# RWKV-7 systems: joined loads, stores and inverse tiles, and the lower triangles stored from ScalarE

## The chip, the cores and the metric

The kernel runs on one core of a Trainium2 chip, as one launch. The metric is device time in microseconds, the median of three runs. TensorE (PE; its weight loads are listed as PEld), VectorE (DVE), ScalarE (ACT) and GpSimd (POOL) compute; SyncE (SP) issues the DMAs in this kernel. All of them run their own instructions in order and wait for each other by semaphores.

## What is computed

One inference step of a two-layer decoder trunk in float32: layer 0 is a gated DeltaNet, layer 1 is RWKV-7 time mixing. 1104 tokens go through it at once: 8 sequences of 8 sample tokens, 16 meta tokens, and 1024 prompt tokens. The change touches layer 1 only. Its recurrence, per head of 64 channels:

```python
kk = l2norm((k * k_k).reshape(B, T, H, N))
k = k * (1.0 + (a - 1.0) * k_a)
decay = jnp.exp(-jnp.exp(w))
b_h = kk * a_h
def step(S, inp):
    S = (S * d_t[:, :, None, :]
         + jnp.einsum('bhvk,bhk->bhv', S, -kk_t)[..., None] * b_t[:, :, None, :]
         + v_t[..., None] * k_t[:, :, None, :])
    return S, jnp.einsum('bhvk,bhk->bhv', S, r_t)
```

It is followed by a GroupNorm per head, a bonus term, a SiLU gate, the output projection and a final RMSNorm. The states of both token mixers are outputs too.

## The kernel before

Tokens lie along the free axis in three segments of 384, 384 and 336 (`SEGS`). 64 tokens form a chunk, two heads of 64 channels fill the 128 partitions as one of 8 pairs, so a segment of a pair has 6 chunks and there are 24 items: item n is pair n mod 8 of segment n div 8. Within a chunk, the recurrence is solved through the inverse of a unit lower triangular 64x64 matrix per head, which the text calls a system.

Layer 1 has three parts.

*Keys, decays and rates* (`keys_decay_rate`, line 1165). For each pair, the k projection and the two low-rank paths give k, the running sum of log decays cs, and the rate a. Each is stored in DRAM (`kd`, `csd`, `ad`, each 8 x 128 x 1152) and read back later.

*Systems beside projections* (`layer1`, line 1801). A list `todo` holds 24 projections: r, v and z (m = 0, 2, 3) of 8 pairs. A projection (`project`, line 1152) loads two weight tiles on SP, splits each into a high and a low part (ACT, then POOL or DVE, `split`, line 82), runs its products on PE, copies the result on ACT and stores it by SP in `rd`, `vd` or `zd`. After the projections n = 1, 4, 7, 10 and 13, `rwkv_inverse` (line 1293) is called for a batch b of five items (the last batch has four).

For each item of a batch, `rwkv_inverse` takes the tiles `cs`, `a`, `k`, which were loaded one item ahead by `rwkv_load`, three DMAs with two buffers each (tiles `sldcs`, `slda`, `sldk`). ACT makes kk (`skk`, line 1268) and the decays and their inverses (`sDp`, `siD`, lines 1277 and 1278). DVE makes α, kk times the decay (`sal`, one buffer, line 1285), POOL mends its chunk heads (1286, 1288), POOL and DVE turn kk into bk, kk times a times the inverse decay (1310, 1311). SP stores α in `ald` and bk in `bkd` (1312, 1313). PE multiplies bk by α for 12 chunk-heads into `fL`, and the squares of kk by the half mask `hmask` into `frss`, two partitions by 384. ACT copies `fL` to `sgl` (1322); in segment 0 POOL masks the sample chunk (1324); SP stores it in `rltd` (1325). DVE copies the sums of squares (`rkc`, 1327) and SP stores them in `rssd` (1328).

After the last item, `block_scale` (line 489) reads `rssd` back as a column and as a row of blocks (`invR`, `bblk`), and `inverse_blocks` (line 457) inverts all 32x32 diagonal blocks of the batch at once on DVE: the blocks are read into `invA`, one block a partition, 62 DVE instructions (`invtmp`, `invT`, lines 452 and 454) work one after the other, and the result goes to DRAM (`r_u`, `r_t`) to be read back in matrix layout, as `T1n` (line 480) and as the diagonal blocks of each item's `sTT` (line 486: four loads per item). A `sTT` tile holds one item, 6 chunks by 64; there are three buffers, and two memsets (484) clear a corner of each before its loads. `inverse_merge` (line 506) then makes the off-diagonal block of each item: PE products `mY` and `mU`, a DVE scaling between them, an ACT copy after them. POOL scales the finished `sTT` (1336) and SP stores it in `ttd` (1337).

*The wave* (`wave`, line 1841). Systems and projections being done, the items go through the chunk recurrence as a skewed wave with PE's order written by hand. `rwkv_front` (line 1340) prepares an item: five loads (`fldcs`, `fldk`, `flda`, one buffer each, `fldr`, `fldv`, two each), α and bk from `ald` and `bkd` into `AR` and `BK` (1360, 1361), the inverse from `ttd` into `rTT` (1351). In segment 0, the sample states are read (`sn`, eight loads, line 1588) and written (`out_s_rwkv`, eight stores, 1636) for each pair.

The tile framework places the semaphores from the tiles' uses, and orders each engine's instructions by a planning pass over the whole program, save PE in the wave. A DMA issue takes its place in the order of the engine that issues it.

Of the kernel before, what the change touches and what calls it, by code (L numbers as in the profile page):

```python
# [11 lines left out]
ALU = mybir.AluOpType  # L12
# [23 lines left out]
class Builder:  # L36
# [76 lines left out]
    def consts(self):  # L113
# [15 lines left out]
        self.hmask = t(cp, [128, 2], "hmask")  # L129
        nc.gpsimd.memset(self.hmask, 0.0)  # L130
        for h in (0, 1):
            nc.gpsimd.memset(self.hmask[64 * h:64 * h + 64, h:h + 1], 1.0)
# [324 lines left out]
    def inverse_blocks(self, name, ltd, scale_blk, pool, TT, T1n, L21, nth):  # L457
# [7 lines left out]
        A = self.t(pool, [128, 1024], "invA", 2)[0:nb]  # L465
# [746 lines left out]
    def rwkv_masks(self, ap, first=False):  # L1212
# [14 lines left out]
        if first:  # L1227
            self.m_strs2 = t(ap, [128, 64], "m_strs2")
            mask(self.m_strs2, True)
            return  # L1230
# [17 lines left out]
    def rwkv_open(self):  # L1248
        self.rk2 = self.t(self.cp, [128, 144], "rk2")
        self.csd, self.ad, self.rd, self.vd, self.zd, self.kd = (self.dram([8, 128, 1152], n) for n in  # L1250
                                                                 ("csd", "ad", "rd", "vd", "zd", "kd"))
        self.ttd, self.ald, self.bkd = (self.dram([24, 128, 384], n) for n in ("ttd", "ald", "bkd"))

    def rwkv_load(self, n, pool, tag, names):
# [4 lines left out]
        for nm in names:  # L1259
            d = {"cs": self.csd, "a": self.ad, "r": self.rd, "v": self.vd, "k": self.kd}[nm]  # L1260
            ld[nm] = t(pool, [128, 384], tag + "ld" + nm, 2 if nm in "rv" or tag == "s" else 1)
            nc.sync.dma_start(ld[nm], d[p][:, c0:c0 + 384])
        return ld

    def rwkv_keys(self, p, ld, pool, tag):

        nc, t = self.nc, self.t
        kk = t(pool, [128, 384], tag + "kk", 2)
# [3 lines left out]
    def rwkv_decays(self, ld, pool, tag):  # L1272
# [4 lines left out]
        self.act(Dp[:, 1:385], ld["cs"], AF.Exp, scale=-self.DEC)  # L1277
        self.act(iD, ld["cs"], AF.Exp, scale=self.DEC)
# [14 lines left out]
    def rwkv_inverse(self, b, pool):  # L1293
# [4 lines left out]
        ltd, ssd = self.dram([nth, 128, 64], f"rltd{b}"), self.dram([nth, 128], f"rssd{b}")  # L1298
        for q, n in enumerate(items):
            s, p = divmod(n, 8)  # L1300
            names = ("cs", "a", "k")
# [6 lines left out]
            al = t(pool, [128, 6, 64], "sal", 1)  # L1308
            self.alpha(al, kk, Dp, s, nc.vector)
            nc.gpsimd.tensor_tensor(kk, kk, ld["a"], op=ALU.mult)  # L1310
            nc.vector.tensor_tensor(kk, kk, iD, op=ALU.mult)
            nc.sync.dma_start(self.ald[n], al.rearrange("p c k -> p (c k)"))
            nc.sync.dma_start(self.bkd[n], kk)
            gp = self.ps("f", 2, "L")
            ssp = self.ps("f", 2, "rss")
            for c in range(6):
                for h in (0, 1):
                    a = 64 * h
                    self.mm(gp[a:a + 64, 64 * c:64 * c + 64], kk[a:a + 64, 64 * c:64 * c + 64], al[a:a + 64, c, :])
            self.mm(ssp[0:2, 0:384], self.hmask, sq)  # L1320
# [656 lines left out]
```

## Time and profile before

| | us |
|---|---|
| median of three runs | 2365.65 (2362.40 to 2366.57) |
| the profiled execution | 2362.64 |
| its span, first to last instruction | 2360.9 |
| PE busy in the span | 2167.1 (92%) |
| DVE busy | 1571.2 (67%) |
| ACT busy | 1282.6 (54%) |
| POOL busy | 949.4 (40%) |

The page also gives the mean granted clock of TensorE, 0.964 of full speed, and 308.89 MB moved by DMA, 131 GB/s on average. All DMA issues of the program come from SP.

How to read the lines below. A group line has the kernel line, engine, operation, the tiles it writes and reads (`out<-in`, with the first letter of a PSUM tag in front of a PSUM tile's name, so `fL` is tile `L` in the banks tagged `f`), their shapes, the count, and times. A line of a tile's view has the shortest, median and longest instruction in ns, then the first and last start in us. `SPq` marks an issue on SP's queue; its time is that of the issue, not of the transfer. A wait line has who waited, for whom, the total in us, how often, and the longest. `issue` as a releaser means that the profile shows nothing that the engine waited for. In a timeline, a row is start, duration, and in brackets the engine's idle time just before and what ended it. PE's busy time is modelled from pipelined matmuls and includes time at a lower clock.

### The profile page before, as it was taken

How to read it: one execution, taken by the hardware profiler on the slowest of the kernel's cores; microseconds unless marked ns; L12 is line 12 of the kernel's file. 1: busy time of each engine (PE TensorE's matmuls, PEld its weight loads, DVE VectorE, ACT ScalarE, POOL GpSimd, SP SyncE). 2: the span in 40 equal slices, each digit the busy share in tenths (PEclk: the TensorE clock that was granted, in tenths of full speed). 3: DMA queues.
4: the chain of work that ended last, by engine and by line, in shares of the span. 5: the costliest groups of instructions: out<-in, count | busy, mean ns of one | idle time of the engine just before them, and what ended most of it. 6: DMA issues, size and time to landing. Idle time of an engine off the chain costs nothing. (4 is left out here: it accounts for less than half of the span.)

```text
span 2360.9 us, 54503 instructions
## 1 busy us (share of the span) xinstructions
PE 2167.1 (92%) x19737; PEld 1961.9 (83%) x19737; DVE 1571.2 (67%) x4219; ACT 1282.6 (54%) x3599; POOL 949.4 (40%) x1318
## 2 busy tenths in 40 slices
PE   6989999999999999999999999999888888899886
PEld 5888989889898989898989998887777866778775
DVE  6878677685858686774345833479878456667754
ACT  5455545564656555456333746646444355677763
POOL 3445333443435353434232523446445423344433
PEclk9999999999999999999999999998999998999998
DMA  3423332323233333335152145577774654677753
GB/s 113 107 76 104 88 94 78 101 75 105 78 101 91 90 102 88 109 90 184 48 163 83 52 163 175 182 199 197 188 181 130 178 160 143 178 220 227 215 153 126
DMA packets 499719, 308.89 MB, mean 131 GB/s; under 512 B 208089, under 2 KB 484826, under 8 KB 499450
## 3 DMA queue, kind: packets, MB, share of 16 engines
q1 hardware_dynamic: 499450, 305.41, 45.6%
q8 instruction: 156, 2.56, 0.5%
q14 instruction: 113, 0.93, 0.1%
HBM read 209.97 MB, written 95.33 MB: 129 GB/s over the span
## 5 line engine op out<-in xcount | busy, mean ns | idle before, releaser
L90 POOL TENSOR_TENSOR wlo<-wraw,whi 128x512 fp32r<-128x512 f32 (+2 forms) x252 | 332.4, 1322 | 359.8 <-ACT whi L86 334.4
L76 PE MATMUL d<-xc,whi 128*128 128x384 f32 (+2 forms) x910 | 260.2, 344 | 8.1 <-ACT whi L86 3.6
L86 ACT CAST whi<-wraw 128x512 fp32r<-128x512 f32 (+2 forms) x252 | 151.7, 603 | 138.8 <-PE dq L76 50.7
L419 DVE SCALAR_TENSOR_TENSOR cvy<-raw,cw,cvy 128x408 f32<-128x408 f32 (+2 forms) x288 | 178.3, 632 | 15.7 <-ACT cvy L62 13.8
L452 DVE TENSOR_TENSOR invtmp<-invA,invT 72x31 f32<-72x31 f32 (+31 forms) x403 | 172.7, 429 | 18.7 <-POOL invT L447 8.0
L76 PEld LDWEIGHTS d<-xc,whi 128*128 128x128 f32 (+1 forms) x910 | 168.9, 193 | 15.2 <-ACT whi L86 4.7
L454 DVE TENSOR_TENSOR invT<-invT,invtmp 72x31 f32<-72x31 f32 (+31 forms) x403 | 172.3, 428 | 6.6
L76 PE MATMUL dz<-xc,whi 128*128 128x384 f32 (+1 forms) x480 | 149.4, 343 | 0.0
L76 PE MATMUL dv<-xc,whi 128*128 128x384 f32 (+1 forms) x480 | 146.8, 335 | 0.0
L76 PE MATMUL d<-xa,whi 128*128 128x384 f32 (+3 forms) x450 | 141.4, 348 | 4.1 <-DVE xa L90 2.8
L76 PE MATMUL d<-xc,wlo 128*128 128x384 f32 (+2 forms) x428 | 143.9, 345 | 0.7 <-POOL wlo L90 0.7
L868 POOL TENSOR_SCALAR Sb<-Sb,eglb 128x128 f32<-128x128 f32 x128 | 80.4, 645 | 87.6 <-DMA Sb<-in_state_gdn 36.6
L76 PE MATMUL dz<-xa,whi 128*128 128x384 f32 (+1 forms) x288 | 100.3, 348 | 0.0
L76 PE MATMUL dv<-xa,whi 128*128 128x384 f32 (+1 forms) x288 | 99.9, 347 | 0.1
L76 PEld LDWEIGHTS d<-xa,whi 128*128 128x128 f32 (+1 forms) x450 | 85.2, 194 | 12.8 <-issue 5.2
L76 PEld LDWEIGHTS dz<-xc,whi 128*128 128x128 f32 x480 | 89.5, 192 | 0.8
L76 PEld LDWEIGHTS dv<-xc,whi 128*128 128x128 f32 x480 | 88.6, 188 | 0.5 <-issue 0.4
L76 PE MATMUL d<-xa,wlo 128*128 128x384 f32 (+3 forms) x252 | 86.6, 344 | 0.0
L62 ACT ACTIVATE o<-rA,gcol 128x128 f32<-128x128 f32 x128 | 46.6, 372 | 72.6 <-DVE S L779 72.0
L76 PE MATMUL d<-xh,wlo 128*128 128x384 f32 (+1 forms) x256 | 83.9, 343 | 2.0 <-POOL wlo L90 2.0
L76 PEld LDWEIGHTS d<-xc,wlo 128*128 128x128 f32 (+1 forms) x428 | 82.1, 194 | 4.0 <-issue 1.9
L76 PE MATMUL d<-xh,whi 128*128 128x384 f32 (+1 forms) x256 | 84.5, 344 | 0.5 <-ACT whi L86 0.5
(509 smaller groups left out, 7012.3 us busy)
## 6 DMA issues: line engine op xcount, KB each, us to landing
wraw<-in_gdn_w_in SPq DMA_DIRECT2D x96, 256.0 KB
wraw<-in_rwkv_w_rkvz SPq DMA_DIRECT2D x80, 256.0 KB
Sb<-in_state_gdn SPq DMA_DIRECT2D x64, 256.0 KB
wraw<-in_rwkv_w_o SPq DMA_DIRECT2D x40, 256.0 KB
E<-drow SPq DMA_DIRECT2D x24, 384.0 KB
attn<-drow SPq DMA_DIRECT2D x24, 384.0 KB
wraw<-in_gdn_w_out SPq DMA_DIRECT2D x36, 256.0 KB
out_s_gdn<-Sb SPq DMA_DIRECT2D x32, 256.0 KB
```

Source lines behind the costliest of these rows:

```text
L62: return self.nc.scalar.activation(out, in_, func, bias=bias, scale=scale, **kw)
L76: self.nc.tensor.matmul(out, lhsT, rhs, start=start, stop=stop)
L86: nc.scalar.copy(hi, x)
L90: e.tensor_tensor(lo, x, hi.bitcast(F32), op=ALU.subtract)
L419: nc.vector.scalar_tensor_tensor(y[:, 0:wd], raw[:, k:k + wd], cw[k], y[:, 0:wd], op0=ALU.mult, op1=ALU.add)
L452: nc.vector.tensor_tensor(tmp, A[:, j, j + 1:32].unsqueeze(2).broadcast_to([nb, n, m]), Tv[:, j, 0:m].unsqueeze(1).broadcast_to([nb, n, m] ...
L454: nc.vector.tensor_tensor(Tv[:, j + 1:32, 0:m], Tv[:, j + 1:32, 0:m], tmp, op=ALU.subtract)
L868: nc.gpsimd.tensor_scalar(Sb[:, u], Sb[:, u], self.eglb[:, hv, 4 * g + u:4 * g + u + 1], None, op0=ALU.mult)
```

## The change

Five edits, all in layer 1:

1. The DRAM copies of cs, a and k become one tensor `cakd` (8 x 128 x 3 x 1152), and those of r and v one tensor `rvd`. Writers use slices as before; `rwkv_load` reads all three (two) in one DMA into one tile. The system loads one tile per item instead of three, the front two instead of five.
2. α and bk share one SBUF tile `ab` (tag `sal`, one buffer) and one DRAM tensor `abd`; one store after bk replaces the two. `kk` has one buffer instead of two.
3. The sums of squares: `hmask` has 32 columns, three products of 128 columns write partitions 0, 32 and 64 of one bank, one copy of 96x128 puts them in a tile `kc` for the whole batch, and six stores after the batch's last item write `rssd`.
4. The store of the lower triangles to `rltd` is issued from ScalarE for segments 1 and 2 and stays on SP for segment 0, whose sample chunk POOL masks.
5. One tile `TA` of 30 chunks with one buffer takes the place of the items' `sTT`; `inverse_blocks` fills it by four loads and two memsets per batch. `invA` has one buffer instead of two. `rwkv_inverse` is called after the projections 0, 3, 6, 9 and 12.

```diff
-        A = self.t(pool, [128, 1024], "invA", 2)[0:nb]
+        A = self.t(pool, [128, 1024], "invA", 1)[0:nb]
...
-        self.csd, self.ad, self.rd, self.vd, self.zd, self.kd = (self.dram([8, 128, 1152], n) for n in
-                                                                 ("csd", "ad", "rd", "vd", "zd", "kd"))
-        self.ttd, self.ald, self.bkd = (self.dram([24, 128, 384], n) for n in ("ttd", "ald", "bkd"))
+        self.cakd, self.rvd, self.zd = (self.dram([8, 128, n, 1152], m) for n, m in ((3, "cakd"), (2, "rvd"), (1, "zd")))
+        self.csd, self.ad, self.kd = (self.cakd[:, :, x] for x in range(3))
+        self.rd, self.vd = (self.rvd[:, :, x] for x in range(2))
+        self.zd = self.zd[:, :, 0]
+        self.ttd, self.abd = self.dram([24, 128, 384], "ttd"), self.dram([24, 128, 768], "abd")
...
-        for nm in names:
-            d = {"cs": self.csd, "a": self.ad, "r": self.rd, "v": self.vd, "k": self.kd}[nm]
-            ld[nm] = t(pool, [128, 384], tag + "ld" + nm, 2 if nm in "rv" or tag == "s" else 1)
-            nc.sync.dma_start(ld[nm], d[p][:, c0:c0 + 384])
+        for g in names:
+            d = {"cak": self.cakd, "rv": self.rvd}[g]
+            x = t(pool, [128, len(g), 384], tag + "ld" + g, 1 if g == "cak" and tag == "f" else 2)
+            nc.sync.dma_start(x, d[p][:, :, c0:c0 + 384])
+            for j, nm in enumerate(g):
+                ld[nm] = x[:, j]
...
+        kc = t(pool, [96, 5, 128], "rkc", 1)
...
-            al = t(pool, [128, 6, 64], "sal", 1)
+            ab = t(pool, [128, 2, 384], "sal", 1)
+            al, bk = ab[:, 0].rearrange("p (c k) -> p c k", k=64), ab[:, 1]
             self.alpha(al, kk, Dp, s, nc.vector)
             nc.gpsimd.tensor_tensor(kk, kk, ld["a"], op=ALU.mult)
-            nc.vector.tensor_tensor(kk, kk, iD, op=ALU.mult)
-            nc.sync.dma_start(self.ald[n], al.rearrange("p c k -> p (c k)"))
-            nc.sync.dma_start(self.bkd[n], kk)
+            nc.vector.tensor_tensor(bk, kk, iD, op=ALU.mult)
+            nc.sync.dma_start(self.abd[n], ab.rearrange("p x k -> p (x k)"))
...
-            self.mm(ssp[0:2, 0:384], self.hmask, sq)
+            for g in range(3):
+                self.mm(ssp[32 * g:32 * g + 32, 0:128], self.hmask, sq[:, 128 * g:128 * g + 128])
...
-            nc.sync.dma_start(ltd[6 * q:6 * q + 6].rearrange("c q i -> q c i"), gl)
-            kc = t(pool, [2, 384], "rkc", 1)
-            nc.vector.tensor_copy(kc, ssp[0:2, 0:384])
-            nc.sync.dma_start(ssd[6 * q:6 * q + 6].rearrange("c (h i) -> h c i", h=2), kc.rearrange("h (c i) -> h c i", c=6))
+            (nc.sync if s == 0 else nc.scalar).dma_start(ltd[6 * q:6 * q + 6].rearrange("c q i -> q c i"), gl)
+            nc.vector.tensor_copy(kc[:, q], ssp[0:96, 0:128])
+        sv = ssd.rearrange("(q g c) (h i) -> g h q c i", g=3, c=2, h=2)
+        for g in range(3):
+            for h in (0, 1):
+                nc.sync.dma_start(sv[g, h:h + 1], kc[32 * g + h:32 * g + h + 1, 0:len(items)].rearrange("h q (c i) -> h q c i", c=2))
...
-        TT = [t(pool, [128, 6, 64], "sTT", 3) for _ in items]
+        TA = t(pool, [128, 30, 64], "sTT", 1)
+        TT = [TA[:, 6 * q:6 * q + 6] for q in range(len(items))]
...
-        self.inverse_blocks(f"r{b}", ltd, blk, pool, TT, T1n[:, 0:nth], L21[:, 0:nth], nth)
+        self.inverse_blocks(f"r{b}", ltd, blk, pool, [TA[:, 0:nth]], T1n[:, 0:nth], L21[:, 0:nth], nth)
...
-        ld = self.rwkv_load(P.n, fp, "f", ("cs", "k", "a", "r", "v"))
+        ld = self.rwkv_load(P.n, fp, "f", ("cak", "rv"))
...
-            if n in (1, 4, 7, 10, 13):
-                self.rwkv_inverse((1, 4, 7, 10, 13).index(n), ip)
+            if n in (0, 3, 6, 9, 12):
+                self.rwkv_inverse((0, 3, 6, 9, 12).index(n), ip)
```

More of the change, by code (lines that the diff above doesn't have):

```diff
@@ L128, in consts @@
         nc.gpsimd.memset(self.ones, 1.0)
[L129 to L132, printed above, removed]
         self.bmask = t(cp, [128, 8], "bmask")
@@ L1229, in rwkv_masks @@
             mask(self.m_strs2, True)
+            self.hmask = t(ap, [128, 32], "hmask")
+            nc.gpsimd.memset(self.hmask, 0.0)
+            for h in (0, 1):
+                nc.gpsimd.memset(self.hmask[64 * h:64 * h + 64, h:h + 1], 1.0)
             return
```

15 lines of the change are left out of this document (8 added, 7 removed).

## The prediction

> **What bounds the kernel now.** I read the split of the span into stages first, then who waits for whom inside the stage that the diff edits, then the instructions around single waits. Durations are those of the profiled execution, 2362.64 us with a span of 2360.9.
>
> The first view is five stretches; columns are the length, then busy time of PE, PEld, DVE, ACT and POOL with instruction counts, then granted TensorE clock, DMA share and GB/s.
>
> ```profile
> 1060.00:1330.00 270.00, 260.34 (x1620) 251.09 (x1618) 132.21 (x301) 123.77 (x371) 87.97 (x99) 0.99 0.39 113
> 1330.00:1465.00 135.00, 129.17 (x743) 126.47 (x742) 55.70 (x80) 74.15 (x152) 44.41 (x56) 0.97 0.44 141
> 1465.00:1860.00 395.00, 358.17 (x3307) 317.53 (x3308) 287.96 (x586) 200.70 (x432) 191.37 (x273) 0.93 0.66 179
> 1860.00:2361.00 501.00, 426.46 (x5983) 357.83 (x5981) 306.48 (x1016) 299.27 (x855) 192.70 (x213) 0.94 0.60 179
> ...
> 1640.20:1646.00 5.80, 3.51 (x29) 2.14 (x30) 5.63 (x9) 3.13 (x8) 4.30 (x5) 0.72 0.75 231
> 1748.90:1758.80 9.90, 5.79 (x35) 4.42 (x36) 9.64 (x20) 2.79 (x8) 6.21 (x8) 0.66 0.74 198
> ```
>
> 1465 to 1860 holds the systems (`rwkv_inverse`) beside the r, v and z projections; 1860 to the end is the wave. TensorE sets the pace in both, but with holes: 395 - 358.2 = 36.8 us idle in the systems' stage, and a clock of 0.93, worth 0.07 x 395 = 27.7 us. The two belong together. The last two rows begin at a hole of PE (2.38 and 4.14 us, below): the clock falls to 0.72 and 0.66, which costs 0.28 x 5.8 = 1.6 and 0.34 x 9.9 = 3.4 us on top. Holes of 6.5 us cost 5.0 us of clock, so I price an idle microsecond of PE at 1.77. In these holes DVE is busy 5.63 of 5.8 and 9.64 of 9.9: it carries the chain that PE waits for.
>
> Next, the waits from 1460 to 1890: engine, line, releaser, then total us, times, longest.
>
> ```profile
> PE fL L76 <- DVE skk L1311: 9.8, 5, 4.1
> PE mU L76 <- issue: 4.7, 3, 2.9
> PE mY L76 <- DMA T1n<-r_t: 4.1, 2, 3.8
> PE d L76 <- ACT whi L86: 3.6, 2, 2.8
> PE mY L76 <- issue: 2.9, 1, 2.9
> ...
> POOL sTT L484 <- DMA ttd<-sTT: 25.0, 11, 5.6
> DVE sal L1285 <- PE fL L76: 20.5, 5, 4.8
> DVE skk L1311 <- POOL skk L1310: 16.8, 9, 3.4
> DVE bblk L502 <- DMA bblk<-rssd: 7.6, 3, 3.3
> ```
>
> Most holes of PE are matmuls of the systems, not projections. Behind them stands a chain: POOL sits 25.0 us in front of the memsets of `sTT`, because only three buffers serve five items and the store to `ttd` must land; its next work, the product `skk` of L1310, comes late, DVE waits 16.8 us for it, and PE 9.8 us for DVE. One such place:
>
> ```profile
> 1739.79 1.01 POOL L1310 TENSOR_TENSOR skk<-skk,slda 128x384 f32<-128x384 f32 x1
> 1746.92 0.54 POOL L484 MEMSET sTT<- 32x192 f32 x2 [2.38 <-DMA ttd<-sTT]
> 1749.52 1.58 POOL L1310 TENSOR_TENSOR skk<-skk,slda 128x384 f32<-128x384 f32 x1
> ...
> 1743.62 0.39 SPq L1337 DMA_DIRECT2D ttd<-sTT  x1
> ...
> 1753.01 0.87 PE L76 MATMUL fL<-sal,skk 64*64 64x64 f32 x11 [4.14 <-DVE skk L1311]
> ```
>
> The store is issued at 1743.62, the memset starts at 1746.92: 3.3 us from issue to freed buffer.
>
> **The change part by part.** The rows that price it (min/median/max ns):
>
> ```profile
> L1262 SPq DMA_DIRECT2D sldcs<-csd x24: 319/400/1271, 1470.7 to 1716.9; - x24
> L1312 SPq DMA_DIRECT2D ald<-sal x24: 319/332/493, 1479.1 to 1750.9; - x24
> L1313 SPq DMA_DIRECT2D bkd<-skk x24: 319/380/1585, 1481.8 to 1752.9; - x24
> L1325 SPq DMA_DIRECT2D rltd<-sgl x24: 366/384/2267, 1501.9 to 1757.1; - x24
> L1328 SPq DMA_DIRECT2D rssd<-rkc x24: 241/264/583, 1501.3 to 1758.3; - x24
> L486 SPq DMA_DIRECT2D sTT<-r_u x96: 302/439/1656, 1592.0 to 1841.2; - x96
> L1361 SPq DMA_DIRECT2D BK<-bkd x24: 523/557/1327, 1857.2 to 2241.1; - x24
> ...
> L1327 DVE COPY rkc<-frss x24: 537/546/547, 1500.4 to 1757.8; 2x384 f32<-2x384 f32 x24
> L1602 DVE COPY rkst<-drsr x8: 275/279/292, 1879.6 to 2009.8; 128x128 f32<-128x128 f32 x8
> L1311 DVE TENSOR_TENSOR skk<-skk,siD 128x384 f32<-128x384 f32 x24 | 16.1, 670 | 16.8 <-POOL skk L1310 16.8
> L1286 POOL COPY sal<-skk 128x6 f32<-128x6 f32 x24 | 7.4, 308 | 31.1 <-DVE sal L1285 24.1 <-DMA sTT<-r_u 7.0
> L484 POOL MEMSET sTT<- 32x192 f32 x48 | 12.1, 252 | 26.6 <-DMA ttd<-sTT 25.0
> L446 POOL MEMSET invT<- 120x1024 f32 (+1 forms) x5 | 4.8, 954 | 10.3 <-DMA r_t<-invT 9.0 <-ACT xa L86 1.3
> 1508.35 0.81 PE L76 MATMUL frss<-sgl,hmask 128*2 128x384 f32 x2
> 1516.43 0.81 PE L76 MATMUL frss<-sgl,hmask 128*2 128x384 f32 x2
> 1894.97 1.08 PE L76 MATMUL drsw<-ue,BT 128*64 128x512 f32 x4 [0.40 <-DVE xss L1611]
> ```
>
> *One tile for five items' inverses.* 96 loads become 20 (four a batch), 48 memsets become 10, and the waits between items go, since the next batch's memsets find stores long landed. Memsets of 32x960 are nearest to the 0.95 us of 120x1024: 9.5 us instead of 12.1. The 25.0 us of POOL waits feed the 9.8 us of PE at fL, worth 9.8 x 1.77 = 17.3 us at most. DVE's own load keeps part of it, and POOL still waits for other things: I take half, -9 (bounds 0 and -17). For mU and mY PE idles 4.7 + 4.1 + 2.9 = 11.7 us. The round trip through DRAM in front of mY stays; only mU's 4.7 x 1.77 = 8.3 us can gain. Against it, the first item now waits until all five are in: 480 KB instead of 96, at the stage's 179 GB/s 2.7 us instead of 0.5, 2.2 later in five batches, +11 idle and +19 with the clock if nothing covers it. Value -2, bounds -8 and +19.
>
> *Sums of squares.* The copy from PSUM goes from 2x384 at 0.546 us to 96x128, nearest the 128x128 copy at 0.279: 24 x 0.27 = 6.4 us less on DVE, the engine that PE waits for in the holes; half of it on the path, -3 (0 to -6). The one product of 384 columns (0.81 us, two instructions) becomes three of 128 columns into partitions 0, 32 and 64. One after the other they cost the same 0.81; the drsw row shows four instructions of 512 columns, into two halves of the partitions, in 1.08 us, while two of 384 take 0.81, so neighbours overlap and up to half goes. 24 x 0.2 = -5; bounds: +2 (four more weight loads each, 24 x 0.08) and -10.
> The Trainium skill, page TensorEngine Tiling (Array Packing), section Available Configurations, goes further: products of up to 32 output columns can run on four independent strips of the array. By that rule the three would take a third of 0.81 us, an estimate of -13 us instead of -5; no row of this trace shows three strips at once.
>
> *The row stores gathered at the end.* Five stores of a batch, four of them early, become six behind its last item: 6 x 0.26 - 0.26 = 1.3 us later for `invR` and `bblk`, 6.6 in all. DVE already waits 7.6 us for `bblk` in three batches. PE is behind it only through the inverse's chain: +2 (0 to +7).
>
> *Fewer issues on SP.* 48 loads x 0.40 + 24 stores x 0.33 + 76 loads x 0.44 + 16 `rltd` stores moved x 0.38 - 6 x 0.26 = 65 us of issue time. A joined load has three pieces a row; between 0.40 and the 0.56 of `BK` (six pieces), 0.45 is fair. SP is no bound: it mostly stands at semaphores of other engines. What it can free is weights that arrive late: PE loses 3.6 us to `whi`, at 1.77 6.4. Value -2 (0 to -6). The 16 moved stores put 0.38 us each on ACT, 6 us on an engine busy 200.7 of 395, right behind its own copy of `gl`; they free SP from standing at that copy: nothing. Without ACT's slack, it would be 6 us.
>
> *Call one projection earlier.* Each batch passes one projection's two weight loads, three stores and two POOL splits, which now queue behind its own issues; the order on each engine is re-planned anyway. Nothing, covered by the projections that follow every batch; without that cover a shift would cost at most PE's longest wait for `whi`, 2.8 us, per batch.
>
> *The joined `ab` tile, one buffer.* α and bk leave in one store, after bk. α of the next item must now wait for that landing, 3.3 us by the rows above, where today α's store leaves 2.7 us before that of bk (first issues at 1479.1 and 1481.8). `kk` is no longer stored, so ACT's wait for it goes. Value +2, and up to 24 x 1.5 = +36 (rival below).
>
> *The wave.* 5 loads to 2, 24 x (5 x 0.40 - 2 x 0.45) = 26 us of SP. The sample pairs are the place where it could matter:
>
> ```profile
> 1917.10 0.62 SPq L1262 DMA_DIRECT2D fldr<-rd  x1
> 1919.33 3.02 SPq L1588 DMA_DIRECT2D sn<-in_state_rwkv  x4
> ...
> 1911.42 0.69 DVE L1618 TENSOR_TENSOR ue<-UV,bmask 128x512 f32<-128x512 f32 x1 [4.62 <-DMA out_s_rwkv<-ue]
> 1912.85 1.97 PE L76 MATMUL drsw<-ue,BT 128*64 128x512 f32 x4 [4.69 <-DVE xss L1611]
> ```
>
> PE waits there behind DVE for the `out_s_rwkv` stores, which the change leaves; and SP has a pause of 1.6 us (1917.72 to 1919.33) in each round. Value -2 (0 to -9, 1.1 us in eight pairs).
>
> **Sum.** -9 - 2 - 3 - 5 + 2 - 2 + 2 - 2 = -19 us: 2362.64 - 19 = 2343.6 as a profiled execution. The median, 2365.65, lies 3.0 above it, so 2346.6, rounded 2347.
>
> **Rivals.** *The store of `ab` becomes the wait.* Per item bk (0.67), α of the same size, POOL's two steps (0.3 + 1.6), 3.3 us from issue to landing and 1.1 for the second 192 KB (at 179 GB/s) make 7.6 us, where items of a batch follow each other every 8.1 us early on (frss at 1508.35 and 1516.43). As soon as DVE or POOL slow down, α stands at the head of DVE's queue, the inverse's 62 steps a batch queue behind it, and PE behind these. Decisive where issue to landing passes 4.4 + 0.5 = 4.9 us. 1.5 us on each of 24 items is 36 us of DVE; half of it on PE's path, +18, and the gains on POOL and DVE are eaten while frss's -5 stays: 2365.65 + 13 = 2379. For it: DVE is the busy engine in the holes, and 20.5 us of α's waits are already there. Against: `kk` frees sooner, and the slack is there in most batches.
> The Trainium skill, page DMA: Bandwidth & Descriptors, section Anatomy of one DMA, puts about 2 us of fixed time on a DMA, most of it the receipt of the last write, longest into HBM: it speaks for this rival, and by its figure alone, an estimate, the landing would take 1.3 us less than the trace's 3.3.
>
> *The joined inverse loads land late*: +19 for mU in place of -2, the rest as summed: 2347 + 21 = 2368, slower by a hair.
>
> *The holes only move.* The transfers were hidden, the order of PE against the chains comes out as holey as now: 2366.
>
> *The holes close.* -17, -8, -6, -10, -6, -9 with the losses of +4: -52, 2314.
>
> **Chances.** Forecast 0.46, closing holes 0.13, no change 0.12, late inverse loads 0.10, `ab` store 0.19. 0.2% is 4.7 us, about what a measurement of this kernel tells from nothing. Faster takes the first two and a little of the third, 0.60; same 0.12, with the late loads' near half; slower 0.28 holds the `ab` case, the other half, and reorderings that fall badly. The forecast's own range is 2330 to 2360; to leave out no more than 2 in 10 it reaches 2322 (most of the closing holes beyond it) and 2378 (half of the `ab` case).
>
> **What would show it.** Right: POOL's wait for `ttd` near 0, fL's wait below 5 us, PE idle in the systems' stage near 25 us with a clock above 0.94, `rkc` copies near 0.28 us, frss near 0.6 us an item. Wrong: α of `sal` waiting for the store to `abd` (rival one), mU waiting for `sTT` once a batch (rival two), or equal idle time under other names (rival three). Should the sample pairs' round of about 20 us shorten by more than 1 us, I mis-sized SP there.

## The result, and the profile after

The changed kernel takes 2374.71 us (median of 10 runs, 2365.66 to 2378.81), the kernel before, run beside it, 2365.58 (10 runs, 2354.81 to 2373.28). The ratio is 1.0035, 95% interval 1.0018 to 1.0052: 4 to 12 us slower. The profiled execution of after took 2378.81 us with a span of 2376.9 and a mean clock of 0.964. It lies 4 us above its median, and 8.8 us of its distance to the profile of before have already arisen when layer 1's low-rank paths end (1479.6 against 1470.8 us). Up to there both kernels do the same work, apart from where in DRAM the stores of cs, a and k go, and over the profiles of all kernels of this document this point lies anywhere from 1465.9 to 1482.5 us; so I compare stages, not times from the start.

The stretch of the systems, cut at the same times as before (length; busy time of PE, PEld, DVE, ACT, POOL; clock; DMA share; GB/s):

```profile
1465.00:1860.00 395.00, 349.29 (x3227) 318.50 (x3226) 281.54 (x570) 200.94 (x432) 179.88 (x217) 0.93 0.62 173
```

POOL is 11.5 us less busy in the systems' stretch, and so is DVE by 6.4, as the diff intends. PE is idle for 45.7 us there instead of 36.8. Since the kernels are shifted against each other, stretches cut at events say more. From the end of the low-rank paths to the first product of the wave's front (`fG`) the systems take 414.9 us instead of 400.6. The wave behind them takes 482.4 instead of 489.5, so the 16.0 us between the two spans are 8.8 ahead of the systems, 14.3 in them and -7.1 in the wave. Where these 14.3 us sit shows when the stage is cut once more at the last product of a projection. Same columns; before, then after:

```profile
1600.00:1861.20 261.20, 233.51 (x2428) 205.85 (x2427) 205.56 (x429) 121.39 (x262) 130.33 (x179) 0.93 0.66 175
1861.20:1871.40 10.20, 5.58 (x30) 4.99 (x29) 6.14 (x8) 3.93 (x8) 5.62 (x7) 0.83 0.65 200
```

```profile
1600.00:1866.30 266.30, 233.14 (x2366) 213.34 (x2364) 211.50 (x436) 128.82 (x277) 127.34 (x128) 0.93 0.61 167
1866.30:1894.50 28.20, 14.66 (x222) 13.03 (x222) 10.61 (x19) 7.82 (x20) 12.57 (x29) 0.68 0.76 209
```

The last row of each is the time between the last projection and the wave. Before it is 10.2 us with 30 products; after it is 28.2 us with 222, of which PE is idle for 13.5 and slowed to a clock of 0.68. The 18 us more are the whole loss of the stage and a little beyond it: the part ahead of this tail, which has 192 products less, got shorter by 3.7 us only, 386.7 instead of 390.4. **The systems have outlived the projections that cover them.** PE's timeline at that place:

```profile
1865.94 0.34 PE L76 MATMUL d<-xl,whi 128*128 128x384 f32 x1
1870.36 1.25 PE L76 MATMUL mY<-T1n,L 32*32 32x32 f32 x24 [4.08 <-issue]
...
1878.88 1.15 PE L76 MATMUL mU<-sTT,invY 32*32 32x32 f32 x24 [0.55 <-DVE invY L514]
```

The merge of the fifth batch (`mY`, `mU`) runs alone on PE after the last projection. In the kernel before the last `mU` ends at 1850.6, 10.6 us ahead of the last projection's end.

Why it is late shows in two views. The waits from 1460 to 1890, with the rows that answer to those of before:

```profile
DVE sal L1289 <- DMA abd<-sal: 25.1, 8, 6.6
...
DVE bblk L498 <- DMA bblk<-rssd: 10.8, 3, 7.0
...
PE fL L76 <- DVE sal L1317: 10.0, 9, 2.7
PE mU L76 <- DVE invY L514: 9.2, 9, 2.4
POOL sTT L480 <- DMA ttd<-sTT: 8.5, 2, 6.9
...
PE mY L76 <- issue: 4.1, 1, 4.1
...
PE mY L76 <- DMA T1n<-r_t: 2.6, 2, 1.9
...
PE mU L76 <- DMA sTT<-r_u: 1.1, 1, 1.1
```

POOL's 25.0 us are down to 8.5, but PE's wait at `fL` is as long as before (10.0 against 9.8); its waits at `mU` and `mY`, 17.0 us in all, take the place of 11.7 before, mostly under other names; and DVE now stands 25.1 us in front of α for the store of `ab`. The second view is the timeline between two batches of the inverse, before and then after. The row of `invT` on 31 columns is the last of the 62 steps of a batch, the row of `invtmp` on 31 columns the first of the next:

```profile
1650.46 1.84 SPq L469 DMA_DIRECT2D invA<-rltd  x2
...
1658.56 1.23 DVE L470 TENSOR_TENSOR invA<-invA,bblk 120x1024 f32<-120x1024 f32 x1
...
1661.95 0.13 DVE L454 TENSOR_TENSOR invT<-invT,invtmp 120x31 f32<-120x31 f32 x1
...
1666.56 0.99 DVE L452 TENSOR_TENSOR invtmp<-invA,invT 120x31 f32<-120x31 f32 x1 [3.37 <-POOL invT L447]
```

```profile
1734.18 0.19 DVE L450 TENSOR_TENSOR invT<-invT,invtmp 120x31 f32<-120x31 f32 x1
...
1734.40 1.93 ACT L468 COPY invA<-invT 120x1024 f32<-120x1024 f32 x1 [2.38 <-DVE invT L450]
...
1736.35 0.34 SPq L471 DMA_DIRECT2D r_u<-invA  x1
...
1740.69 2.72 SPq L482 DMA_DIRECT2D sTT<-r_u  x4
1743.45 1.82 SPq L465 DMA_DIRECT2D invA<-rltd  x2
...
1749.38 1.23 DVE L466 TENSOR_TENSOR invA<-invA,bblk 120x1024 f32<-120x1024 f32 x1 [0.63 <-DMA rltd<-sgl]
1750.64 0.19 DVE L448 TENSOR_TENSOR invtmp<-invA,invT 120x31 f32<-120x31 f32 x1
```

Before, the next batch's blocks are loaded 11.6 us ahead of the end of the running one, and even scaled before it. After, the one `invA` is still the source of the store to `r_u`; the next load is issued 7.1 us behind that store, and the next chain begins 16.3 us behind the last. Of the 7.1 us at most 4.3 are the landing of the store, since at 1740.69 SP already issues loads that read `r_u`; for the rest the load of `invA` stands behind these four. The four gaps between the five chains (end of the 62nd step to the first of the next batch) add up to 39.8 us before (22.9, 4.5, 7.0 and 5.4) and 78.0 after (25.9, 20.5, 16.3 and 15.4).

### The profile page after: what moved, and what is told of

It reads as the page before. It is cut to its first block, busy times and chain, and to the rows that moved or that the text cites. A ratio compares the mean times of both kernels' runs of the same rounds, so it can differ in the third digit from the quotient of the medians.

```text
span 2376.9 us, 54215 instructions
## 1 busy us (share of the span) xinstructions
PE 2165.9 (91%) x19833; PEld 1969.8 (83%) x19833; DVE 1571.6 (66%) x4219; ACT 1282.0 (54%) x3599; POOL 943.6 (40%) x1280
## 5 line engine op out<-in xcount | busy, mean ns | idle before, releaser
L76 PE MATMUL d<-xa,whi 128*128 128x384 f32 (+3 forms) x450 | 141.9, 350 | 2.1 <-DVE xa L90 1.7
```

Of the source, the lines that this page charges most:

```text
L76: self.nc.tensor.matmul(out, lhsT, rhs, start=start, stop=stop)
```

## The experiments

Eighteen kernels, each timed in five rounds beside the kernel before; ratios are to that kernel, with the 95% interval. These theories stand in the expectations. **A**: the landing of the joined `ab` store holds up α. **R**: the row stores gathered at the end delay the next inverse. **M**: any edit only reshuffles the planned order. From e5 on, **B**: one `invA` buffer makes the batches serial, and **T**: the tile of five itself costs. Each stage length below is from one profiled execution.

### e1, e2, e3, e4: one part undone, or one part alone

e1 is the changed kernel with α and bk in tiles and stores of their own:

```diff
-            ab = t(pool, [128, 2, 384], "sal", 1)
-            al, bk = ab[:, 0].rearrange("p (c k) -> p c k", k=64), ab[:, 1]
+            al, bk = t(pool, [128, 6, 64], "sal", 1), kk
...
-            nc.sync.dma_start(self.abd[n], ab.rearrange("p x k -> p (x k)"))
+            nc.sync.dma_start(self.ald[n], al.rearrange("p c k -> p (c k)"))
+            nc.sync.dma_start(self.bkd[n], bk)
```

> The changed kernel with alpha and bk stored apart again (alpha tile with one buffer, bk in kk with two, two stores, two DRAM tensors); all else as changed. Theory A (the landing of the joined ab store stands in front of DVE): DVE's wait for the store falls from 25.1 us to under 3 us, the systems' part (end of the low-rank products to the first fG) shrinks by 10 us or more, and the time falls to about 2364 us, 0.999 of the kernel before. Theory R (the six row stores gathered behind a batch's last item make the inverse late): the waits for invR and bblk stay, the time stays at 2372 to 2376. Theory M (any edit only reshuffles the planned order): anything within 6 us of 2374, with DVE's wait gone and another in its place.

2367.32 us against 2365.42, ratio 1.0013 [0.9997, 1.0030]. DVE's wait for `abd` is gone, and the systems take 402.0 us instead of 414.9. A is supported, though the interval overlaps that of the changed kernel. Since `kk` has two buffers again here, its share is not told apart from that of the store. The tail is as long as in the changed kernel:

```profile
1844.30:1871.00 26.70, 15.43 (x223) 13.87 (x222) 10.59 (x19) 9.09 (x20) 12.18 (x29) 0.62 0.79 212
```

The gaps between the chains of the inverse are as long too, 78.5 us in all, for `invA` still has one buffer. But the part ahead of the tail takes 375.3 us, 15 less than in the kernel before. So a long tail is not a loss by itself: the products in it are missing from the part ahead, and what counts is whether that part gets shorter by as much.

e2 is the changed kernel with the rows stored per item again (one product of 384 columns, one copy of 2x384, one store):

```diff
-            for g in range(3):
-                self.mm(ssp[32 * g:32 * g + 32, 0:128], self.hmask, sq[:, 128 * g:128 * g + 128])
+            self.mm(ssp[0:2, 0:384], self.hmask[:, 0:2], sq)
```

> The changed kernel with the sums of squares as in the kernel before (one product of 384 columns, a copy of 2x384, one row store per item); all else as changed. Theory R: PE's wait of 8.2 us for invR and DVE's 10.8 us for bblk fall to a third, the time falls by 8 us or more, to about 2366. Theory A: DVE's 25 us wait for the ab store stays, the time stays within 3 us of 2374.7; it may rise a little, since DVE gets 6 us of copies back.

2384.66, ratio 1.0088 [1.0069, 1.0106]: slower, not faster. R falls as the cause of the changed kernel's loss. Why it is slower by 12 us was not tried further; what its profile shows is a longer wait of DVE for the `ab` stores, 38.9 us:

```profile
DVE sal L1289 <- DMA abd<-sal: 38.9, 10, 7.0
```

e3 is the reverse of e1: the kernel before with the joined `ab` alone.

> The kernel before with the joined ab tile alone (one buffer, one store after bk, kk with one buffer). Theory A: DVE waits 15 us or more for the store, and the time rises by 8 us or more, to 2374 or above. Theory R: no rise beyond 3 us, ratio 1.000.

2373.02, ratio 1.0028 [1.0010, 1.0046]. The rise of some 7 us fits A, but DVE's wait in the row below is about half of the 15 us that A had named. `kk` has one buffer here, as in the change, so the loss is that of both:

```profile
DVE sal L1285 <- DMA abd<-sal: 8.3, 4, 4.2
```

e4 is the kernel before with the tile of five and one `invA` buffer:

```diff
-        A = self.t(pool, [128, 1024], "invA", 2)[0:nb]
+        A = self.t(pool, [128, 1024], "invA", 1)[0:nb]
...
-        TT = [t(pool, [128, 6, 64], "sTT", 3) for _ in items]
+        TA = t(pool, [128, 30, 64], "sTT", 1)
+        TT = [TA[:, 6 * q:6 * q + 6] for q in range(len(items))]
```

> The kernel before with the one inverse tile of five items alone (four loads and two memsets a batch, invA with one buffer). By my forecast's step: POOL's 25 us wait for the store to ttd goes, PE's wait for fL halves, 8 us faster or more, 2357. If the late joined load decides instead, mU waits for sTT about 2 us in each batch and the time is 2366 or above. If the holes only move, 2363 to 2368.

2374.59, ratio 1.0049 [1.0033, 1.0066]. The edit that I had priced at -11 us costs 12, though it does what I said to POOL, whose wait for `ttd` falls from 25.0 us to this:

```profile
POOL sTT L484 <- DMA ttd<-sTT: 6.4, 1, 6.4
```

### e5 to e8: the tile or the buffer

e5 is the kernel before with the first line of e4's diff only.

> The kernel before with invA in one buffer instead of two, nothing else. Theory B (with one buffer, a batch's blocks can be read only after the last batch's inverse has been stored and has landed, so each DVE chain starts some 14 us after the end of the one before instead of at once): the gap between chains goes from about 0 to 4 us to 12 us or more, the last chain ends 20 us later or more, and the time rises by 7 us or more, to 2373. Theory T (the joined tile itself costs, by late loads for mU): no change, within 3 us of 2365.4.

2379.33 against 2360.01, ratio 1.0095 [1.0076, 1.0114]: one buffer count costs 22 us, more than the whole change. Its tail after the last projection, from the same view as above:

```profile
1848.00:1884.40 36.40, 15.36 (x224) 13.81 (x224) 14.81 (x33) 9.10 (x19) 11.57 (x31) 0.57 0.55 148
```

36.4 us instead of 10.2, at a clock of 0.57; the gaps between its chains sum to 85.2 us.

e8 is the kernel before with the tile of five and both `invA` buffers. Room comes from writing the inverse decays in place of cs and from `invR` sharing the tag of `rkc`.

> The kernel before with the one inverse tile of five items, but invA in two buffers; the room for it comes from the systems' inverse decays written in place of cs and from invR sharing the tag of rkc. Theory B: the chains follow each other within 5 us and the time is at or below that of the kernel before, 2365 or less (my forecast's step would give 2357). Theory T: it stays near e4's 2374.6.

2358.09, ratio 0.9997 [0.9982, 1.0013]. T falls: the tile costs nothing, and it brings nothing either. Tail and POOL's wait:

```profile
1859.30:1866.80 7.50, 4.87 (x33) 4.38 (x31) 3.87 (x7) 3.93 (x8) 4.24 (x7) 1.00 0.67 205
```

```profile
POOL sTT L484 <- DMA ttd<-sTT: 9.3, 2, 7.4
```

e6 is the changed kernel with item tiles of `sTT` and two `invA` buffers (e4's diff reversed).

> The changed kernel with invA in two buffers and an inverse tile per item (three buffers) as before; joined loads, joined ab, gathered rows, stores from ScalarE and the early calls stay. Theory B or T: the gaps between chains shrink to 5 us or less, the time falls by 8 us or more, to 2367 or below. Theory A alone: the ab wait stays and the time stays at 2372 or above.

2380.04, ratio 1.0087 [1.0067, 1.0106]. A miss: in the changed kernel the second buffer, bought by going back to three `sTT` buffers, recovers nothing. α still waits 24.7 us for `abd`, POOL 23.1 us for `ttd` again, and the tail is 30.9 us long. The chains are no closer to each other either: their gaps are 27.5, 22.1, 30.5 and 7.1 us, 87.2 in all. SP's timeline in the longest of them, which ends at 1751.81, shows why a second buffer did not help there:

```profile
1728.60 7.51 SPq L482 DMA_DIRECT2D sTT<-r_u  x12
1736.15 3.74 SPq L1336 DMA_DIRECT2D rssd<-rkc  x5
1739.94 1.62 SPq L465 DMA_DIRECT2D invA<-rltd  x2
...
1743.85 0.85 SPq L496 DMA_DIRECT2D bblk<-rssd  x2
```

The last item's sums are copied at 1723.83, but five of the six gathered row stores stand on SP behind twelve loads of `sTT`, and the loads of `invA` and `bblk` stand behind those stores. DVE then waits for `bblk` until 1746.02. So this gap, which theory B would put down to `invA`, comes from the gathered rows and the order on SP.

e7 is e6 with α and bk apart.

> As e6_no_tile, and alpha and bk stored apart: joined loads, gathered rows, stores from ScalarE and the early calls are what is left of the change. If the costs of ab (7 us) and of tile with invA (9 us) add up, 2374.7 - 16 = 2359 or below, faster than the kernel before; if both only opened the same hole at the end of the systems, 2364 to 2367.

2375.75, ratio 1.0064 [1.0044, 1.0085]. A miss too: neither `ab` nor one `invA` is in it, and it is slower by 15 us. Something else in the change costs. The waits that grew against the kernel before:

```profile
ACT skk L62 <- DMA bkd<-skk: 27.9, 8, 4.9
...
DVE bblk L498 <- DMA bblk<-rssd: 21.5, 4, 8.2
```

### e9 to e12: the earlier call, and both losses undone

Two theories for what e6 and e7 left open: **C**, the earlier call costs, and **AB**, only A and B do. e9 is the changed kernel, called as before:

```diff
-            if n in (0, 3, 6, 9, 12):
-                self.rwkv_inverse((0, 3, 6, 9, 12).index(n), ip)
+            if n in (1, 4, 7, 10, 13):
+                self.rwkv_inverse((1, 4, 7, 10, 13).index(n), ip)
```

> The changed kernel with the systems' batches called after projections 1, 4, 7, 10 and 13 again, as before the change; all else as changed. Theory C (calling a batch one projection earlier costs, and this is the unexplained +0.6% of the kernel without the tile and with alpha and bk apart): 6 us or more below the changed kernel, ratio to before at or under 1.001. Theory AB (the loss lies in invA's one buffer and in the landing of ab, the call is free as I predicted): within 4 us of the changed kernel, ratio 1.002 to 1.005.

2380.95 against 2361.20, ratio 1.0089 [1.0066, 1.0112]. Both expectations miss: the earlier call is worth some 0.5% to the changed kernel. Without it the tail is 34.3 us long:

```profile
1850.20:1884.50 34.30, 15.65 (x222) 13.95 (x222) 16.14 (x36) 8.93 (x18) 10.98 (x29) 0.61 0.63 170
```

e10 is the changed kernel with α and bk apart and two `invA` buffers, tile of five and all the rest kept. To make room, kk and the inverse decays overwrite the loaded k and cs, and `invR` shares `rkc`'s tag.

> The changed kernel with alpha and bk stored apart and two invA buffers; the tile of five, the joined loads, the gathered rows, the earlier call and rltd from ScalarE stay. To make room, kk and the inverse decays are written in place of the loaded k and cs, and invR shares the tag of rkc. Theory AB: after loses 9, of which ab gave 7 to 8 and invA 10 to 19, so it ends below before: 2350 to 2359, ratio 0.994 to 0.998; DVE's inverse chains start 4 to 7 us after each other. Theory C: the earlier call still costs, ratio 1.001 or more.

2364.20, ratio 1.0022 [1.0007, 1.0038]. Theory AB missed by 5 to 14 us, and so did its chains 4 to 7 us apart: the gaps are 22.5, 17.2, 16.7 and 3.9 us. Against e1 (1.0013), which has one `invA` buffer and no tiles written in place, the second buffer has brought nothing that can be told. The tail is down to 16.7 us, but two other waits are long, ACT's for the joined load and DVE's for the blocks of sums:

```profile
ACT sldcak L62 <- DMA sldcak<-cakd: 41.0, 12, 6.2
...
DVE bblk L498 <- DMA bblk<-rssd: 23.4, 4, 8.9
```

e11 is e10 with the calls of before.

> As e10 (alpha and bk apart, two invA buffers) and the batches called after projections 1, 4, 7, 10 and 13. Theory AB: the same as e10 within 4 us. Theory C: 6 us or more below e10, at a ratio of 0.995 or less.

2365.88, ratio 1.0027 [1.0011, 1.0042], the same as e10, so here the call's place does not matter. Why it does in the changed kernel was not tried further: the gaps between the chains add up to 60 us in e10 and 70 in e11, so these two have not become free of them.

e12 is the kernel before with gathered rows and tile of five, two `invA` buffers, and kk and the inverse decays in place.

> The kernel before with only the gathered rows (three products of 128 columns, one copy of 96x128, six stores a batch) and the tile of five with two invA buffers; loads and stores of alpha, bk, cs, a and k as before, kk and inverse decays in place of the loaded tiles. If the gathered rows' gain of 10 us in the changed kernel is their own: 2353 to 2358, ratio 0.995 to 0.997. If it was only the cure of a wait that the changed kernel has and before has not: 0.998 to 1.001.

2366.09, ratio 1.0025 [1.0009, 1.0041], slower where I expected 5 to 10 us of gain or no change. The gain that e2 seemed to show for the gathered rows does not carry to this kernel; DVE's wait for `bblk` is 21.5 us. Whether the in-place tiles add to it was not tried apart.

### e13 to e18: the planned order, and the parts left

The parts did not add up, and every edit makes the planning pass lay out another order, so I tried whether that order alone costs (theory L; R stands in these two expectations for its opposite). e13 writes the product into `frss` ahead of the twelve into `fL`, e14 the squares behind α; neither changes any work, buffer or size. In e13's trace PE, DVE, ACT, POOL and SP all run another order than in the kernel before; in e14's SP issues the same DMAs in the same order, and the others differ.

> The kernel before with frss's product written ahead of fL's twelve: the same work, buffers and waits, but the planning pass lays out another order on every engine of the systems' stage (PE, DVE, ACT, POOL and SP). Theory L (a good part of the +2 to +10 us of e6, e7 and e10 to e12 is what another planned order costs against the order that before happens to have): 4 us or more away from before, slower more likely, ratio 1.002 to 1.008. Theory R (buffers and landings alone set the time): within 4 us, ratio 0.998 to 1.002.

> The kernel before with the squares (ACT) written behind alpha instead of ahead of it: again the same work, buffers and waits, with a planned order that differs less than e13's. Theory L: between 0.999 and 1.005, away from 1. Theory R: 0.998 to 1.002.

e13: 2357.41 against 2362.02, ratio 0.9996 [0.9978, 1.0015]. e14: 2360.11, ratio 0.9999 [0.9978, 1.0020]. L has no support: two other orders of the same work are worth nothing measurable, within 0.2% either way. So losses of 0.5 to 0.9% are hardly the order's luck; those of 0.2 to 0.3% lie near what these two intervals leave open. One profile also differs from the next: the systems took 395.8 us in e13 and 397.2 in e14, against the 400.6 of the kernel before.

e15 is the kernel before with the gathered rows alone.

> The kernel before with the gathered rows alone (three products of 128 columns, one copy of 96x128 per item, six stores a batch). As I summed it in the prediction (copy -3, products -5, later stores +2): 2355, ratio 0.996 to 0.999. If the six stores behind the last item make DVE wait for bblk (21.5 to 23.4 us in e10 and e12, 7.6 before): +3 to +10 us, ratio 1.001 to 1.004. Theory L adds up to 8 us of either sign.

2363.13, ratio 1.0005 [0.9985, 1.0025]. Neither a gain nor a loss; the wait for `bblk` has tripled from 7.6 us:

```profile
DVE bblk L498 <- DMA bblk<-rssd: 22.9, 3, 8.6
```

e16 is the kernel before with the joined loads alone (DRAM tensors `cakd` and `rvd`, one tile and one load each); e17 keeps the joined load in the systems and goes back to five loads in the wave.

> The kernel before with the joined loads alone (one DMA for cs, a and k, one for r and v). Prediction's steps: fewer issues on SP, none of them a bound: -4 to 0 us, ratio 0.998 to 1.000, the sample pairs up to 6 us shorter (160 instead of 166 us, as in the changed kernel). If ACT waits for the larger load to land (41.0 us in e10): DVE and PE behind it, +2 to +8 us, ratio 1.001 to 1.004.

> The kernel before with the joined load of cs, a and k in the systems alone; the wave loads its five pieces one by one, from the same joined DRAM tensors. e16 (both joined) was 0.54% slower, with the systems' stage 5.7 us and the wave 6 us longer in its profile. If the loss is the systems' (ACT waiting for one large landing): ratio 1.003 to 1.006. If it is the wave's (DVE waiting for fldrv) or in both: 0.999 to 1.003.

e16: 2372.52 against 2362.02, ratio 1.0054 [1.0035, 1.0074]. e17: 2367.67 against 2359.32, ratio 1.0038 [1.0018, 1.0059]. The joined load costs. By the expectation of e17 the loss is the systems', but the two intervals overlap, and the profiles put half of it elsewhere: the systems take 406.4 us in e16 and 406.3 in e17 against 400.6, and the wave 495.5 and 495.2 against 489.5, though e17's wave loads its pieces one by one. What lengthens that wave was not tried; both kernels have the joined DRAM tensors. From e16's tile view of `sldcak`, its load, what its readers waited for, and who waited for them:

```profile
L1264 SPq DMA_DIRECT2D sldcak<-cakd x24: 524/530/607, 1470.8 to 1735.3; - x24
...
  DMA sldcak<-cakd: 17.6, 7
...
  DVE skk L1315: 21.3, 7
```

In the kernel before, the readers of k and cs wait 1.4 and 0.5 us for their loads; here they wait 17.6. PE's wait at `fL` grows with it, from 9.8 to this:

```profile
PE fL L76 <- DVE skk L1315: 17.3, 12, 3.1
```

e18 is the kernel before with the stores to `rltd` of segments 1 and 2 on ScalarE.

> The kernel before with the stores to rltd of segments 1 and 2 issued from ScalarE, alone. As predicted (hidden in ACT's slack): within 4 us, ratio 0.998 to 1.002. If the 16 issues hold up ACT's copies that PE or DVE wait for: +3 to +8 us, ratio 1.001 to 1.004.

2356.77 against 2359.32, ratio 0.9985 [0.9970, 1.0000]: as predicted, or a gain of a few microseconds.

## Why the prediction was wrong, step by step

The forecast was 19 us faster; it came out some 8 us slower, on the other side. The parts, each alone in the kernel before, in us of 2362:

| part | summed as | measured alone (95%) |
|---|---|---|
| tile of five, two `invA` buffers (e8) | -11 | -1 (-4 to +3) |
| `invA` from two buffers to one (e5) | not priced | +22 (+18 to +27) |
| tile and one `invA` (e4) | -11 | +12 (+8 to +16) |
| joined `ab`, `kk` in one buffer (e3) | +2 | +7 (+2 to +11) |
| gathered rows: copy, products, stores (e15) | -6 | +1 (-4 to +6) |
| joined loads (e16) | -4 with the wave's | +13 (+8 to +17) |
| `rltd` from ScalarE (e18) | 0 | -4 (-7 to 0) |
| call one projection earlier (after against e9) | 0 | about -13 |

The parts above the last add to +29 us (e4, e3, e15, e16, e18), the earlier call takes 13 off (6 to 20, from two separate comparisons), and 8 are measured. What is missing lies within the intervals, or hides because the parts delay the same chain.

So the sum failed in four places. The gain from POOL's wait, with the rest of the tile's -11, was not there. The joined loads, priced by SP's issues at -4, cost 13. The `ab` store, at +2, costs 7. And one buffer of `invA`, which costs 22 alone, had no term. How these share the changed kernel's 8 us is open, since the parts do not add up.

The measured time lies near the slow end of the widest range that I gave (2322 to 2378), and that end stood there for half of the `ab` case. That it covers this result is partly luck: neither the cost of one `invA` buffer nor that of the joined loads is in it.

**One step is missing from the sum.** The diff's first changed line takes a buffer from `invA`, I listed it under the change, and the sum has no term for it. The price could have been read from the profile of before. The second buffer is what lets the load at 1650.46 run ahead of the chain that ends at 1662.08. Without it, per batch, ACT's copy (2.0 us), the store's issue and landing, the two loads' issue and landing (together 13.0 us from 1736.35 to 1749.38 in after) and the scaling (1.23) lie one after the other: 16.3 us in the gap shown. e5 shows the price by itself, 22 us, and e8 that the tile without this loss costs nothing. How much of it the changed kernel pays is not shown. e1 keeps one buffer and the same gaps and is 0.13% slower than the kernel before, and no kernel with the second buffer back and the rest of the change left in place (e6, e10) gained by it; in e6's longest gap the chain waits for the gathered sums instead.

**The cover that I named ran out.** I priced the earlier call at nothing, "covered by the projections that follow every batch". The profile of before has the last `mU` only 10.6 us ahead of the last projection's end. Any delay of the chain beyond that falls on a PE that has little else, at a clock of 0.57 to 0.68. It fits that e5, with the longest tail, loses most, and that the earlier call, a head start of one projection, is worth 13 us to the changed kernel. It is not the whole account: e1 has a tail of 26.7 us and loses next to nothing, and e16 loses 13 us with a tail of 11.3.

**POOL's wait was no bound.** I took half of 17.3 us as the gain of freeing POOL. In e8 its wait falls from 25.0 to 9.3 us, DVE's wait for POOL's product from 16.8 to 7.3, and yet PE's wait at `fL` stays (10.4 against 9.8) and so does the time; in after POOL waits 8.5 us and PE's wait at `fL` is unchanged. This is the largest gain of the sum, and the step from POOL's wait to PE's is the one that failed. That bk then waits for its place in DVE's own queue is how I read it; it was not tried.

**Rival one's wait came true.** I gave the point at which α's wait for the `ab` store decides: 4.9 us from issue to landing. SP's and DVE's timelines of after:

```profile
1515.70 0.58 SPq L1318 DMA_DIRECT2D abd<-sal  x1
...
1524.01 0.56 SPq L1318 DMA_DIRECT2D abd<-sal  x1
...
1521.19 0.56 DVE L1289 TENSOR_TENSOR sal<-skk,sDp 128x384 f32<-128x384 f32 x1 [5.64 <-DMA abd<-sal]
...
1529.26 0.56 DVE L1289 TENSOR_TENSOR sal<-skk,sDp 128x384 f32<-128x384 f32 x1 [5.31 <-DMA abd<-sal]
```

From issue to the next α are 5.5 and 5.3 us here, and 6.6 for the item behind them. My +2 came from the 3.3 us of a store of 192 KB with nothing added for the second 192 KB; the rival had that term, and the sum should have had it too. The rival's price of +18 was too high: e3 has +7 (2 to 11). Of the 25.1 us that α waits for the store in after, most only replace its wait for PE's products, which falls from 20.5 to 2.1 us. And I wrote that ACT's wait at `kk` goes, since `kk` is no longer stored. It went (6.6 us), but with one buffer of `kk` ACT now waits there 41.8 us for DVE's bk; in the kernel before it waited 26.4 us for bk, one instruction later, at `siD`. What this costs was not tried apart. The Trainium skill (DMA: Bandwidth & Descriptors, Anatomy of one DMA) gives about 2 us as the fixed part of a DMA that GpSimd issues. The stores here are SP's, and no run splits their landing into a fixed part and the rest.

**The products and the copy came out better than summed and gave nothing.** In after:

```profile
1510.82 0.42 PE L76 MATMUL frss<-sgl,hmask 128*32 128x128 f32 x6
...
L1332 DVE COPY rkc<-frss x24: 275/281/289, 1501.7 to 1777.9; 96x128 f32<-96x128 f32 x24
```

0.42 us an item instead of 0.81 (I forecast 0.6). If three in a row took the 0.81, as the sum supposed, this shows that they overlap in part. By the rule of the Trainium skill (TensorEngine Tiling (Array Packing), Available Configurations) all three would run at once, an estimate of 0.27 us; the trace does not agree. The copy is the 0.28 that I named. In e15 nothing of it is left in the time: six stores behind the batch's last item make DVE wait for `bblk`, 22.9 us. My bound for that was +7 us, from 1.3 us of issue; the row of the stores in after, `rssd<-rkc`, has 0.70 us an issue, not 0.26:

```profile
L1336 SPq DMA_DIRECT2D rssd<-rkc x30: 576/699/847, 1540.5 to 1781.4; - x30
```

**Fewer issues were not free.** I costed the joined loads by SP's issue time alone, in which SP is no bound. What the readers wait for is the landing. Two readings of e16's 17.6 us offer themselves: one DMA of 576 KB lets its first reader start only when the last byte of cs, a and k is there; or three tiles come free one by one and a joined one only after its last reader (POOL's product), so the next load starts later. The traces show the second at work. The load of k in the kernel before, then the joined one in e16, each below the reader that frees its tile:

```profile
1500.24 0.63 ACT L62 ACTIVATE skk<-sldk,pcol 128x384 f32<-128x384 f32 x1
1500.89 0.32 SPq L1262 DMA_DIRECT2D sldk<-kd  x1
...
1517.24 1.01 POOL L1314 TENSOR_TENSOR skk<-skk,sldcak 128x384 f32<-128x384 f32 x1 [3.19 <-ACT sgl L62]
1518.28 0.53 SPq L1264 DMA_DIRECT2D sldcak<-cakd  x1
```

The two longest of e16's waits, 4.7 and 3.5 us, follow loads that SP issued later still, 8.7 and 10.2 us after POOL's product; ahead of the second it was at twelve loads of `sTT` for 8.9 us. How much is left for the size of the transfer was not tried. For the wave's term no gain is shown: between the first and the last `drsw` product lie 135.4 us in after and 141.9 before, but 141.3 in e1, which has the same joined loads. Kernels whose wave is that of before range from 137.0 (e18) to 144.1 us (e4), so little of this needs a cause.

**Rival two did not come.** PE waits for `sTT` at `mU` once, 1.1 us. It waits longer for DVE's `invY`, 9.2 us. **Rival three**, the holes only move, describes the systems up to the last projection well (386.7 against 390.4 us); it had no place for the tail. Of the signs that I had named for the forecast, the copies came as said and `frss` better; POOL's wait near 0, the wait at `fL` below 5 us, PE's idle time of 25 us and a clock above 0.94 did not: 8.5, 10.0, 45.7 and 0.93.

No kernel of these is faster than the one before by more than can be told; e18 comes nearest. The tile with two `invA` buffers and `rltd` from ScalarE, which cost nothing alone, were not tried together; the tile and the gathered rows, which cost nothing alone either, were together 0.25% slower in e12. A second buffer for `ab` was not tried.

## What to carry to other kernels

Before a stage of side work is changed, look where it ends against the work that covers it: 10.6 us of slack was all there was here, and what passed it ran on a half idle PE at a lower clock. That is a loss as far as the covering work does not end earlier by as much. Read every buffer count in a diff as a wait that is added or removed; follow the tile from its last reader's landing to its next load, and multiply by the batches. Joining transfers saves issues, but a joined tile is ready when its last part has landed and free when its last part has been read. Undo a suspected loss in the changed kernel too, and not only do it alone in the old one: here a gap between two chains had one cause in after and another in e6.

## What the hardware showed that I had not expected

Saving DMA issues by the dozen made a kernel slower. The buffer of a store of 192 KB (`ttd`) came free 3.3 us after its issue, that of one of 384 KB (`abd`) after 5.3 to 6.6; but a store of 480 KB (`r_u` in after) had landed at most 4.3 us after its issue, so size alone does not set it. And a kernel whose engines run the same work in another order (e13) took the same time within 0.2%, where one buffer count changed it by 1%.
